# Output projection in products of 512 columns with one bank per chunk of tokens, its weights packed in fours, and the heads' reciprocal norms placed ahead on VectorE

## The chip, the cores and the metric

The kernel runs on one core of a Trainium2 chip. A core has TensorE (matrix products, written PE in the profile; its weight loads are the row PEld), VectorE (DVE), ScalarE (ACT), GpSimd (POOL) and SyncE (SP, which here issues all the transfers), each with its own queue, worked off in order. Matrix products write into PSUM, which has eight banks of 128 partitions x 512 float32 values; all else stands in SBUF or in HBM, and transfers (DMA) move it. The metric is the time of one execution on the device in microseconds; lower is better.

## The reference, cut to what matters

Two layers of an encoder trunk for 512 tokens of width 1024. In each layer one input projection of the residual stream x feeds three branches: a bidirectional state-space scan, differential attention with 8 heads, and cross-attention into 256 memory tokens. Each branch is projected to 1024 channels and weighted by a gate; the sum `merged` goes through one output projection and a layer norm. The lines that the change touches:

```python
o = _diff_attention(q, k, v, lam)
o = _rmsnorm(o, diff_norm_w[layer]) * (1.0 - lambda_init)   # one norm per head and token
y_diff = o.reshape(Bsz, S, DIFF_WIDTH) * jax.nn.silu(dg.astype(jnp.float32))
...
out = jnp.einsum('bsd,de->bse', merged, w_out[layer])
x = _layernorm(DEEPNORM_ALPHA * x.astype(jnp.float32) + out, ln_g[layer], ln_b[layer])
```

## The kernel before

**Arithmetic.** Every operand of a large product is split into a high and a low float32r part (`split`: ScalarE copies the high part, VectorE subtracts to get the low one), and `mm3` makes three products of each pair: low x high, high x low, high x high. Weights come from HBM in units of 128 x 1024 float32 (512 KB): the transfer fills `wr` (two buffers), the split fills `wh` and `wl` (three buffers each). `emit` runs through a plan of units and jobs and keeps loads and splits two units ahead.

**What sets the order.** A planner orders the instructions of each engine: among those that its own model holds ready, the one that stands first in the program goes first. `late(n)` moves the instructions in it n places back for that choice, `late(-n)` n places ahead. Between the first attention unit and `order.close` the queue of TensorE is not planned: it follows the program. All transfers wait in one queue of SyncE.

**The stages of a layer** are `ssd`, `cross`, `diff`, `wout`. In `diff` (from line 785) 35 steps s = 0 to 34 follow each other, each with one weight unit of 24 products of 512 columns (`proj2`): first the jobs `first`, then 12 products, then the jobs `amid`, then 12 products. The attention itself is in the jobs: `scores`, `turn` (transposes), `values`. `values(h, 1)` leaves the squares of head h in a tile of tag `fth` (two buffers), and `sums(h)` adds them up on TensorE; ScalarE copies the sums to `ss` (tile `fs` in the profile). `norm(lo, hi)` then makes the reciprocal norms of heads lo to hi-1 on VectorE: a reciprocal, then a chain of 16 small dependent instructions (`rsqrt` at line 113 is 12 of them; its result is tile `rs_y`).

- `norms`, in the middle of step 30: `norm` for the heads 0 to 6, a transpose on TensorE, a copy, a store to HBM (`rd`).
- `fin(h)` for h < 7: a transfer spreads the norms of head h from `rd` over 128 partitions into a tile of tag `fth`; VectorE multiplies `sdy` by it; the split gives `dy`, the operand of the branch's projection.
- `last`, in the middle of step 33: `norm` for head 7, whose sums are made at the start of that same step, and at once four products (`rb`, eight instructions on TensorE, named pm<-cst,rs_y) that spread it; `fin(7)` reads `rb` from PSUM.

After step s come the jobs `fin`: heads 0, 1 after step 31; 2, 3 after 32; 4, 5 after 33; 6, 7 after 34. Then `branch_out` projects `dy` in 8 units b(0) to b(7) of 24 products of 512 columns each, and `merged` splits the sum over the branches into the operands of the output projection.

**The output projection** (`wout`, from line 1029). The merged rows of 128 tokens are the operand that is loaded into TensorE, and the weight unit is streamed: `proj_tok` (line 182) makes products of 256 columns, so a unit holds 4 blocks of 128 rows x 256 columns, two units make a quarter of the output's columns, and two chunks of 128 tokens share a bank of tag `pj` (three buffers). When a quarter is complete, VectorE adds the residual (`stt`, line 1071; the residual comes by a transfer in `resid`, tags q1 and k0) and takes the statistics of 256 columns (line 1074). In layer 0 the four chunks go together, 8 units for the next layer's memory keys and values are put between the parts (`FILL`) and 8 more come behind them, and `norm` makes the layer norm and the transposed x for the next layer. In layer 1 (`GROUPS`) chunks 0 and 1 go first, then chunk 2, then chunk 3; the weights stay in SBUF, and `norm_last` writes each group out.

Of the kernel before, what the change touches and what calls it, by code (L numbers as in the profile page):

```python
# [15 lines left out]
ALU = mybir.AluOpType  # L16
# [4 lines left out]
P = 128  # L21
S = 512
D = 1024
KC = D // P
NL = 2
M = 256
EPS = 1e-5
ALPHA = (2 * NL) ** 0.25
# [13 lines left out]

LX, LD = 70, 80

FILL = (0, 2, 0, 2, 0, 4, 0, 0)

# [3 lines left out]
def bc(ap, shape):  # L52
    return ap.broadcast_to(shape)


class Net:
# [137 lines left out]
    def setup(self):  # L194
# [590 lines left out]
    def diff(self, l):  # L785
        nc = self.nc
# [184 lines left out]
        def job(fn, *a):  # L971
            return lambda: fn(*a)
# [10 lines left out]
        units = []  # L983
# [7 lines left out]
        for s, unit in enumerate(units):  # L991
            first = [job(scores, s + 1)] if s + 1 < nst else []
            amid = []
            if s % 4 == 2 and s < nst:
                amid.append(job(values, s // 4, 0))
            if s % 4 == 0 and 0 < s <= nst:
                amid.append(job(values, s // 4 - 1, 1))
            if s < nst:
                amid.append(job(turn, s))
            if s % 4 == 1 and 1 < s <= nst + 1:  # L1000
                first.append(job(sums, s // 4 - 1))
            if s == nst - 2:
# [26 lines left out]
    def wout(self, l, load, fill):  # L1029
# [3 lines left out]
        def begin():  # L1033
            op = self.op = self.fp
            self.rT = self.t(op, [P, 4, D], "dy0", bufs=1)
            if last:
                gb = self.t(op, [P, 4, D], "dy1", bufs=1)
                self.gb = [gb[:, i, :] for i in range(4)]
                nc.sync.dma_start(out=gb[:, 2:, :], in_=self.a["lngb"][l - 1:l].broadcast_to([P, 2, D]))
                nc.sync.dma_start(out=gb[:, :2, :], in_=self.a["lngb"][l:l + 1].broadcast_to([P, 2, D]))  # L1040
            else:
                load(op, "dy1", "rsw", "q0")
            self.st = self.t(op, [P, S], "ro", bufs=1)[:, :96].rearrange("p (c i e) -> p c i e", c=4, i=4)

        def resid(p, c, n):

            r = self.t(self.op, [P, n, 256], ("q1", "k0")[c // 2])
            src = self.a["x"] if l == 0 else self.nd
            e = slice(p * 256, (p + 1) * 256)
            nc.sync.dma_start(out=r, in_=src[c * P:(c + n) * P, e].rearrange("(c p) e -> p c e", c=n))  # L1050
            if l:
                for g, op in ((self.gb[2], ALU.mult), (self.gb[3], ALU.add)):
                    self.tt(r, r, bc(g[:, None, e], [P, n, 256]), op)
            return r

        def part(j, chunks):
            def f(wh=None, wl=None):
                p, half = j // 2, j % 2
                banks = [chunks[i:i + 2] for i in range(0, len(chunks), 2)]
                if half == 0:  # L1060
                    self.res = [resid(p, cs[0], len(cs)) for cs in banks]
                    self.ops = [self.bank(self.pj, "pj") for _ in banks]
                if wh is None:
                    wh, wl = self.wo[j]
                self.wo[j] = wh, wl
                self.proj_tok(half, wh, wl, *self.mg, self.ops, chunks)
                if half:
                    e = slice(p * 256, (p + 1) * 256)
                    for ps, r, cs in zip(self.ops, self.res, banks):
                        n = len(cs)  # L1070
                        self.stt(self.rT[:, cs[0]:cs[0] + n, e], ps[:, :n * 256].rearrange("p (c e) -> p c e", c=n), 0.5 / ALPHA,
                                 r, ALU.mult, ALU.add)
                        for c in cs:
                            nc.vector.bn_stats(out=self.st[:, c, p, :], in_=self.rT[:, c, e])
            return f

        def stats(chunks):
# [88 lines left out]
def pack(x, mem, positions, w_in, conv_w, conv_b, dt_bias, a_log, d_skip, ssd_norm_w, diff_lam, diff_norm_w,  # L1166
# [4 lines left out]
    def units(w):  # L1171
        return w.reshape(KC, P, -1, P).transpose(2, 1, 0, 3).reshape(-1, P, 1024)

    def pairs(w):
        return w.reshape(2, 4, P, -1, 256).transpose(3, 0, 2, 1, 4).reshape(-1, P, 1024)

    wu = []
    for l in range(NL):
        bs = w_br_ssd[l].reshape(4, 4, P, 4, 256).transpose(0, 3, 2, 1, 4).reshape(16, P, 1024)
        wi = np.concatenate([w_in[l][:, :5120], w_in[l][:, 5184:]], axis=1)  # L1180
        wu.append(np.concatenate([
            units(wi[:, :UV * P]), pairs(wi[:, UV * P:UDG * P]), units(wi[:, UDG * P:]),
            units(w_mem_kv[l][:, :D]), pairs(w_mem_kv[l][:, D:]), bs, units(w_br_diff[l]), units(w_br_cross[l]), pairs(w_out[l])]))
    chan = lambda v: v.reshape(-1, P).T
    pk = []
    for l in range(NL):
# [42 lines left out]
```

## Time and profile before

| what | us |
|---|---|
| median of 3 runs | 2241.68 (2237.81 to 2244.03) |
| the profiled execution, its own time | 2240.25 |
| its span, first to last instruction | 2238.5 |
| PE busy in the span | 2173.2 (97%) |
| DVE busy | 1589.9 (71%) |
| ACT busy | 1004.6 (45%) |
| mean granted clock of TensorE | 0.994 of full speed |

The page of the profile gives busy times of the engines, a picture of the span in 40 slices, the chain of work that ended last, and the costliest groups of instructions. A name such as pj<-wh,wT says that the product writes a tile of tag pj and reads tiles of the tags wh and wT; numbers at the end of a tag are left out (wT0 is wT, dy0 is dy). Products on PE are pipelined, so that the durations of neighbouring ones overlap: the time that one takes in a row of them is the distance from start to start. In lists by time, a bracket at the end of a row holds the idle time before it and what ended it.

### The profile page before, as it was taken

Reading aid. Unit: us, or ns where it says so; the run is one execution under the profiler, and the core shown is the slowest. Engines: PE = TensorE matmul, PEld = TensorE weight load, DVE = VectorE, ACT = ScalarE, POOL = GpSimd, SP = SyncE. Lnnn points to the kernel's source line nnn. Section 1 sums busy time; section 2 is a strip of 40 time slices with the busy share of each in tenths; the row PEclk is TensorE's granted clock in tenths of the full one; section 3 lists DMA queues with packets and bytes.
Section 4 is the critical chain, followed back from the end, with each engine's and each line's share of the span. In section 5 each row is a group of like instructions: output and inputs, shape, how many; then the busy total and the mean of one; then the engine's idle time right before and its main releaser. Section 6 shows DMA issues by size and latency. Waiting matters only on the chain.

```text
span 2238.5 us, 30344 instructions
## 1 busy us (share of the span) xinstructions
PE 2173.2 (97%) x11714; PEld 1787.8 (80%) x11714; DVE 1589.9 (71%) x2468; ACT 1004.6 (45%) x1895; POOL 52.9 (2%) x38
## 2 busy tenths in 40 slices
PE   8999999999999999998999999999999999999898
PEld 6777877788888788877996777787788887888678
DVE  7887888758544777765567888888744547777657
ACT  5664545424432555442355564554423325544430
POOL 0000000000000000000000000010100000000000
PEclk9999999999999999999999999999999999999999
DMA  4654444425453222233564545453433332223333
GB/s 148 180 160 144 147 142 138 126 85 190 145 179 115 90 81 82 81 104 108 163 225 115 165 141 151 132 152 122 123 124 118 116 106 85 78 84 90 109 99 128
DMA packets 108278, 283.79 MB, mean 127 GB/s; under 512 B 12588, under 2 KB 17252, under 8 KB 107876
## 3 DMA queue, kind: packets, MB, share of 16 engines
q1 hardware_dynamic: 108132, 281.84, 41.2%
q8 instruction: 92, 1.51, 0.3%
q14 instruction: 54, 0.44, 0.1%
HBM read 255.55 MB, written 17.85 MB: 122 GB/s over the span
## 4 chain that ended last, share of the span: by engine, by line
PE 71%; DVE 14%; DMA 7%; ACT 5%; issue 2%; SPq 0%; POOL 0%; DVEq 0%; POOLq 0%; ACTq 0%
PE pj L103 59%; PE pm L103 9%; DMA ab<-dab 4%; DVE wl L81 2%; PE pt L111 2%; DVE ab L81 2%; DVE acc L84 2%; ACT ab L91 1%; ACT wh L91 1%; DVE y L81 1%; DVE rx L81 1%; PE pt L103 1%; DMA wr<-wu 1%; DMA fth<-rd 1%; DVE yl L84 1%
## 5 line engine op out<-in xcount | busy, mean ns | idle before, releaser
L103 PE MATMUL pj<-xh,wl 128*128 128x512 f32 x1664 | 669.1, 402 | 10.8 <-DVE wl L81 8.9
L103 PE MATMUL pj<-xh,wh 128*128 128x512 f32 x1664 | 660.8, 397 | 0.0
L103 PE MATMUL pj<-xl,wh 128*128 128x512 f32 x1664 | 658.1, 395 | 0.0
L81 DVE TENSOR_TENSOR wl<-wr,wh 128x1024 fp32r<-128x1024 f32 x330 | 404.5, 1226 | 108.3 <-ACT wh L91 107.5
L91 ACT ACTIVATE wh<-wr 128x1024 fp32r<-128x1024 f32 x330 | 347.4, 1053 | 235.3 <-PE pj L103 199.5
L103 PEld LDWEIGHTS pj<-xh,wl 128*128 128x128 f32 x1664 | 314.1, 189 | 90.8 <-issue 18.3
L103 PEld LDWEIGHTS pj<-xh,wh 128*128 128x128 f32 x1664 | 313.7, 189 | 71.6 <-issue 6.0
L103 PEld LDWEIGHTS pj<-xl,wh 128*128 128x128 f32 x1664 | 314.1, 189 | 63.5 <-issue 3.6
L91 ACT ACTIVATE ab<-ab,bias 128x128 f32<-128x128 f32 x512 | 160.7, 391 | 121.9 <-DVE ab L81 121.3
L84 DVE SCALAR_TENSOR_TENSOR acc<-pj,hcw,acc 128x510 f32<-128x510 f32 x192 | 142.4, 743 | 23.8 <-ACT acc L91 22.4
L91 ACT ACTIVATE fpp<-pm,fmx 128x512 f32<-128x512 f32 x128 | 87.9, 687 | 83.4 <-DVE fmx L881 82.6
L881 DVE TENSOR_REDUCE fmx<-pm 128x1 f32<-128x512 f32 x128 | 87.0, 686 | 45.4 <-PE pm L103 45.1
L103 PE MATMUL pj<-yl,wh 128*128 128x512 f32 x256 | 102.3, 400 | 0.8 <-DVE yl L84 0.8
L103 PE MATMUL pj<-yh,wh 128*128 128x512 f32 x256 | 103.1, 403 | 0.0
L81 DVE TENSOR_TENSOR ab<-ab,cst 128x1024 f32<-128x1024 f32 x64 | 86.3, 1349 | 22.9 <-DMA ab<-dab 22.8
L103 PE MATMUL pj<-dy,wh 128*128 128x512 f32 (+1 forms) x384 | 101.9, 354 | 0.0
L103 PE MATMUL pj<-yh,wl 128*128 128x512 f32 x256 | 101.9, 399 | 0.0
L103 PE MATMUL pj<-cy,wh 128*128 128x512 f32 x256 | 78.8, 389 | 0.0
L103 PEld LDWEIGHTS pj<-dy,wh 128*128 128x128 f32 x384 | 68.0, 189 | 10.0
L103 PE MATMUL pj<-wh,xl 128*128 128x256 f32 x256 | 74.8, 292 | 0.0
L103 PE MATMUL pj<-wl,xh 128*128 128x256 f32 x256 | 72.4, 283 | 0.0
L103 PE MATMUL pj<-wh,xh 128*128 128x256 f32 x256 | 72.3, 283 | 0.0
(273 smaller groups left out, 3387.3 us busy)
## 6 DMA issues: line engine op xcount, KB each, us to landing
wr<-wu SPq DMA_DIRECT2D x336, 512.0 KB, 3.6
ab<-dab SPq DMA_DIRECT2D x64, 512.0 KB, 5.7
eb<-deb SPq DMA_DIRECT2D x64, 256.0 KB, 4.8
mkv<-dkv SPq DMA_DIRECT2D x16, 512.0 KB, 4.3
rsw<-rx SPq DMA_DIRECT2D x128, 64.0 KB, 2.0
dgt<-tg SPq DMA_DIRECT2D x18, 256.0 KB, 2.6
dkv<-mo SPq DMA_DIRECT2D x16, 256.0 KB, 4.0
dkv<-q SPq DMA_DIRECT2D x16, 256.0 KB, 3.7
```

Source lines behind the costliest of these rows:

```text
L81: (eng or self.nc.vector).tensor_tensor(out=out, in0=a, in1=b, op=op)
L84: self.nc.vector.scalar_tensor_tensor(out=out, in0=a, scalar=s, in1=b, op0=op0, op1=op1)
L91: self.nc.scalar.activation(out=out, in_=a, func=f, **kw)
L103: self.nc.tensor.matmul(out=out, lhsT=a, rhs=b, start=first, stop=last)
L111: self.nc.tensor.transpose(out=out, in_=x, identity=self.ident)
L881: nc.vector.tensor_reduce(out=mx[:, c:c + 1], in_=ps, axis=AX.X, op=ALU.min)
```

## The change

- **Weights.** `w_out` is packed by `quads`: a unit now holds 2 blocks of 128 rows x 512 columns, and four units make one half of the output's columns.
- **Products.** `out_tok` takes the place of `proj_tok` in `wout`: for each chunk of tokens, two row blocks of three products of 512 columns, into a bank of its own.
- **Banks.** These are of tag `pm` (four buffers) in place of `pj`. A chunk's sum is complete after four units (`quarter` 3); then one `stt` of 512 columns and one `bn_stats` of 512 columns follow for each chunk.
- **Residual.** One transfer for each chunk and half, 128 x 512, in the tags q1, rx (first half) and k0, k1 (second half).
- **Reciprocal norms.** `norm` becomes a job of its own, after step 29 for the heads 0 to 6 and after step 33 for head 7, in `late(-300)`; `spread` (the rest of `norms`) stays in the middle of step 30; `last` holds only the four spreading products and moves to the middle of step 34.
- **The jobs `fin`** now come two after step 32, three after step 33, three after step 34.

```diff
-LX, LD = 70, 80
+LX, LD, LN = 70, 80, 300
...
+    def out_tok(self, quarter, wh, wl, xh, xl, banks, chunks):
+
+        for o, c in zip(banks, chunks):
+            x = slice(c * P, (c + 1) * P)
+            for k in range(2):
+                kk, w = 2 * quarter + k, slice(k * 512, (k + 1) * 512)
+                self.mm3(o, xh[kk][:, x], xl[kk][:, x], wh[:, w], wl[:, w], kk == 0, kk == KC - 1)
...
         def norm(lo, hi):
 
-            n = 4 * (hi - lo)
             s0, ss = self.s0[:, 4 * lo:4 * hi], self.ss[:, 4 * lo:4 * hi]
-            nc.vector.reciprocal(out=s0, in_=s0)
-            self.stt(ss, ss, 1.0 / 128.0, s0, ALU.mult, ALU.mult)
-            self.tt(ss, ss, s0, ALU.mult)
-            self.ts(ss, ss, EPS, ALU.add)
-            r = self.rsqrt(self.fp, ss, n)
-            self.tt(r, r, s0, ALU.mult)
-            return r
-
-        def norms():
+            with self.late(-LN):
+                nc.vector.reciprocal(out=s0, in_=s0)
+                self.stt(ss, ss, 1.0 / 128.0, s0, ALU.mult, ALU.mult)
+                self.tt(ss, ss, s0, ALU.mult)
+                self.ts(ss, ss, EPS, ALU.add)
+                self.r = self.rsqrt(self.fp, ss, 4 * (hi - lo))
+                self.tt(self.r, self.r, s0, ALU.mult)
+
+        def spread():
 
             n = 4 * (KC - 1)
-            r = norm(0, KC - 1)
             pt = self.bank(self.pt, "pt")
-            self.tr(pt[:n, :P], r)
+            self.tr(pt[:n, :P], self.r)
...
         def last():
 
-            r = norm(KC - 1, KC)
+            r = self.r
             self.rb = self.bank(self.pm, "pm")
...
             if s == nst - 2:
-                amid.append(norms)
-            if s == nst + 1:
+                amid.append(spread)
+            if s == nst + 2:
                 amid.append(last)
             step(unit, first, amid)
-            if s >= nst - 1:
-                for h in range(2 * (s - nst + 1), min(2 * (s - nst + 1) + 2, KC)):
-                    self.T(job(fin, h))
+            if s in (nst - 3, nst + 1):
+                self.T(job(norm, *((0, KC - 1) if s < nst else (KC - 1, KC))))
+            for h in {nst: (0, 1), nst + 1: (2, 3, 4), nst + 2: (5, 6, 7)}.get(s, ()):
+                self.T(job(fin, h))
...
-        def resid(p, c, n):
-
-            r = self.t(self.op, [P, n, 256], ("q1", "k0")[c // 2])
+        def resid(p, c):
+
+            r = self.t(self.op, [P, S], (("q1", "rx"), ("k0", "k1"))[p][c // 2])
             src = self.a["x"] if l == 0 else self.nd
-            e = slice(p * 256, (p + 1) * 256)
-            nc.sync.dma_start(out=r, in_=src[c * P:(c + n) * P, e].rearrange("(c p) e -> p c e", c=n))
+            e = slice(p * S, (p + 1) * S)
+            nc.sync.dma_start(out=r, in_=src[c * P:(c + 1) * P, e])
...
-                p, half = j // 2, j % 2
-                banks = [chunks[i:i + 2] for i in range(0, len(chunks), 2)]
-                if half == 0:
-                    self.res = [resid(p, cs[0], len(cs)) for cs in banks]
-                    self.ops = [self.bank(self.pj, "pj") for _ in banks]
+                p, quarter = divmod(j, 4)
+                if quarter == 0:
+                    self.res = [resid(p, c) for c in chunks]
+                    self.ops = [self.bank(self.pm, "pm") for _ in chunks]
...
-                self.proj_tok(half, wh, wl, *self.mg, self.ops, chunks)
...
+                self.out_tok(quarter, wh, wl, *self.mg, self.ops, chunks)
+                if quarter == 3:
+                    e = slice(p * S, (p + 1) * S)
+                    for ps, r, c in zip(self.ops, self.res, chunks):
+                        self.stt(self.rT[:, c, e], ps, 0.5 / ALPHA, r, ALU.mult, ALU.add)
+                        nc.vector.bn_stats(out=self.st[:, c, p, :], in_=self.rT[:, c, e])
...
+    def quads(w):
+        return w.reshape(4, 2, P, -1, 512).transpose(3, 0, 2, 1, 4).reshape(-1, P, 1024)
```

More of the change, by code (lines that the diff above doesn't have):

```diff
@@ L1042, in begin @@
                 load(op, "dy1", "rsw", "q0")
-            self.st = self.t(op, [P, S], "ro", bufs=1)[:, :96].rearrange("p (c i e) -> p c i e", c=4, i=4)
-        def resid(p, c, n):
-            r = self.t(self.op, [P, n, 256], ("q1", "k0")[c // 2])
+            self.st = self.t(op, [P, S], "ro", bufs=1)[:, :48].rearrange("p (c i e) -> p c i e", c=4, i=2)
+        def resid(p, c):
+            r = self.t(self.op, [P, S], (("q1", "rx"), ("k0", "k1"))[p][c // 2])
             src = self.a["x"] if l == 0 else self.nd
-            e = slice(p * 256, (p + 1) * 256)
-            nc.sync.dma_start(out=r, in_=src[c * P:(c + n) * P, e].rearrange("(c p) e -> p c e", c=n))
+            e = slice(p * S, (p + 1) * S)
+            nc.sync.dma_start(out=r, in_=src[c * P:(c + 1) * P, e])
             if l:
                 for g, op in ((self.gb[2], ALU.mult), (self.gb[3], ALU.add)):
-                    self.tt(r, r, bc(g[:, None, e], [P, n, 256]), op)
+                    self.tt(r, r, g[:, e], op)
             return r
@@ L1065, in f @@
                 self.wo[j] = wh, wl
-                self.proj_tok(half, wh, wl, *self.mg, self.ops, chunks)
[L1067 to L1074, printed above, removed]
+                self.out_tok(quarter, wh, wl, *self.mg, self.ops, chunks)
[4 more added lines that the diff above has]
+                        nc.vector.bn_stats(out=self.st[:, c, p, :], in_=self.rT[:, c, e])
             return f
@@ L1182, in pack @@
             units(wi[:, :UV * P]), pairs(wi[:, UV * P:UDG * P]), units(wi[:, UDG * P:]),
-            units(w_mem_kv[l][:, :D]), pairs(w_mem_kv[l][:, D:]), bs, units(w_br_diff[l]), units(w_br_cross[l]), pairs(w_out[l])]))
+            units(w_mem_kv[l][:, :D]), pairs(w_mem_kv[l][:, D:]), bs, units(w_br_diff[l]), units(w_br_cross[l]), quads(w_out[l])]))
     chan = lambda v: v.reshape(-1, P).T
```

## The prediction

> **What bounds the kernel now.** I read the page first, then the stages, then the waits of TensorE, then lists by time.
>
> ```profile
> span 2238.5 us, 30344 instructions
> PE 2173.2 (97%) x11714; PEld 1787.8 (80%) x11714; DVE 1589.9 (71%) x2468; ACT 1004.6 (45%) x1895; POOL 52.9 (2%) x38
> PE 71%; DVE 14%; DMA 7%; ACT 5%; issue 2%; SPq 0%; POOL 0%; DVEq 0%; POOLq 0%; ACTq 0%
> ```
>
> TensorE is busy 2173.2 of 2238.5 us, so all that can be won without removing products is 65.3 us of idle time and what products lose to a slow clock. The stages that the change touches (columns: length, then busy time of PE, PEld, DVE, ACT, POOL, granted clock, share and rate of the transfers):
>
> ```profile
> 985.00:1026.00 41.00, 31.52 (x146) 26.39 (x147) 18.86 (x39) 14.17 (x23) 0.00 (x0) 0.92 0.31 97
> 1068.00:1144.00 76.00, 75.64 (x640) 75.33 (x638) 44.55 (x77) 26.08 (x33) 0.00 (x0) 1.00 0.55 173
> 1144.00:1172.00 28.00, 27.17 (x193) 24.89 (x194) 19.43 (x28) 18.36 (x28) 0.52 (x1) 1.00 0.73 246
> 1172.00:1824.00 652.00, 638.35 (x3127) 510.56 (x3126) 470.69 (x666) 297.35 (x585) 26.82 (x16) 1.00 0.44 132
> ```
>
> The output projection of layer 0 (second row) is bound by TensorE alone. The end of `diff` (first row) is not: 9.5 of 41 us are idle, at a lower clock. The waits of TensorE (total, times, longest) say on whom:
>
> ```profile
> engine line waited for: us in total, times, longest us
> PE pm L103 <- DVE rs_y L81: 16.1, 2, 8.2
> PE pj L103 <- DVE wl L81: 9.9, 5, 6.8
> ```
>
> The largest wait of the kernel is the four products of `last` on the reciprocal norms of head 7, once in each layer. By time, layer 0, then layer 1:
>
> ```profile
> 1002.01 0.95 PE L103 MATMUL pt<-cst,fth 128*128 128x1 f32 x8
> 1005.44 0.39 PE L103 MATMUL pj<-xh,wh 128*128 128x512 f32 x1
> 1013.99 2.08 PE L103 MATMUL pm<-cst,rs_y 128*128 128x128 f32 x8 [8.16 <-DVE rs_y L81]
> 1016.29 0.63 PE L103 MATMUL pj<-xl,wh 128*128 128x512 f32 x1
> 1016.72 0.63 PE L103 MATMUL pj<-xh,wh 128*128 128x512 f32 x1
> 1024.95 0.39 PE L103 MATMUL pj<-dy,wl 128*128 128x512 f32 x1
> ...
> 2121.04 0.39 PE L103 MATMUL pj<-xh,wh 128*128 128x512 f32 x1
> 2129.38 2.08 PE L103 MATMUL pm<-cst,rs_y 128*128 128x128 f32 x8 [7.96 <-DVE rs_y L81]
> 2140.74 0.39 PE L103 MATMUL pj<-dy,wl 128*128 128x512 f32 x1
> ```
>
> The sums of head 7 start at 1002.01, the first half of step 33 ends at 1005.67 (1005.44 + 0.23), and then the queue stands until 1013.99. After that the products come 0.43 us apart (1016.29 to 1016.72) instead of 0.227, for the clock has fallen:
>
> ```profile
> 1014.00:1018.00 4.00, 4.00 (x14) 3.57 (x15) 1.20 (x2) 0.63 (x1) 0.00 (x0) 0.53 0.00 0
> ```
>
> **The change, part by part.**
>
> *1. The wait in `last` (removed).* From the end of the first half of step 33 to the first product of b(0): layer 0, 1024.95 - 1005.67 = 19.28 us; layer 1, 2140.74 - 2121.27 = 19.47. In that time TensorE has 36 products of 512 columns and the eight instructions of `rb` to do. The pitch of warm products, and the cost of a small instruction:
>
> ```profile
> 1068.48 0.28 PE L103 MATMUL pj<-wh,fpp 128*128 128x256 f32 x1
> 1074.08 0.28 PE L103 MATMUL pj<-wh,v 128*128 128x256 f32 x1
> ...
> 992.08 0.44 PE pt L111 x4
> ```
>
> From 1024.95 to 1068.48 are the 192 products of b(0) to b(7): 0.2267 us each. Four transposes took 0.44 us, so eight small instructions come to some 0.9. Needed: 36 x 0.2267 + 0.9 = 9.06 us. Lost: 10.2 and 10.4 us, **20.6 in all**, of which 16.1 are the wait and 4.5 the slow clock behind it. Neither has other work beside it.
>
> The Trainium skill ("TensorE: Matmul & The Clock Gate", section "Part 1: The HAM clock gate") says that an idle window of about 3.4 us halves the clock, and that as long a busy one restores it. The 0.53 over 4 us behind 8.16 us of idle agrees. By that rule a wait that shrinks below 3.4 us loses its slow stretch too.
>
> *2. What is late next: `last` in step 34.* It now stands 24 products later, so TensorE comes to `rb` at 1005.67 + 24 x 0.2267 = 1011.1 (layer 1: 2126.7). VectorE and ScalarE before:
>
> ```profile
> 1004.26 0.16 ACT L91 ACTIVATE fs<-pt 128x4 f32<-128x4 f32 x1
> 1003.88 1.23 DVE L81 TENSOR_TENSOR wl<-wr,wh 128x1024 fp32r<-128x1024 f32 x1 [0.87 <-ACT wh L91]
> 1006.44 0.69 DVE L81 TENSOR_TENSOR sdy<-sdy,fth 128x512 f32<-128x512 f32 x1 [0.74 <-DMA fth<-rd]
> 1007.05 0.16 DVE L84 SCALAR_TENSOR_TENSOR fs<-fs,fs 128x4 f32<-128x4 f32 x1
> 1010.91 0.69 DVE L81 TENSOR_TENSOR sdy<-sdy,fth 128x512 f32<-128x512 f32 x1 [0.45 <-DMA fth<-rd]
> 1013.17 0.69 DVE L81 TENSOR_TENSOR dy<-sdy,dy 128x512 fp32r<-128x512 f32 x1
> 1013.78 0.15 DVE L81 TENSOR_TENSOR rs_y<-rs_y,fs 128x4 f32<-128x4 f32 x1
> ...
> 974.65 0.18 DVE L84 SCALAR_TENSOR_TENSOR fs<-fs,fs 128x28 f32<-128x28 f32 x1
> 979.22 0.19 DVE L81 TENSOR_TENSOR rs_y<-rs_y,fs 128x28 f32<-128x28 f32 x1
> ```
>
> The sums are there at 1004.42. The chain of 16 took 6.9 us (1007.05 to 1013.93), because it started behind a multiply of `fin` that waited for a transfer, and shared VectorE with others of the kind; for the heads 0 to 6 the same 16 took 4.8 us (974.65 to 979.41), with other work between. Bounds for the wait at the new place: below, the chain goes ahead from 1005.1, when the weight split ends, takes 4.8, is done at 9.9: no wait. Above, everything on VectorE stays as it was: 1013.93 - 1011.1 = 2.8 us (2.6 in layer 1). I take 0.5 per layer, nearer the lower end, because three of the multiplies of `fin` now stand behind the chain in the program. **+1.0**; if the cover is gone, +5.4.
>
> Queued behind the chain on VectorE are multiplies and splits of `fin`. The last transferred one ended its split at 1013.86. TensorE now reaches b(0) at 1005.67 + 9.06 = 1014.7 and uses row block k of `dy` after 3k products: block 6 at 1018.8, block 7 at 1019.5. Block 7 follows `rb` (done 1012.0) by a multiply and a split of some 0.7 each: near 1014. So the heads have 5 us in hand, if their transfers don't move. Each of them takes over 3 us and they share two buffers; their places in the plan go back by up to a step (5.44 us), their readiness doesn't. That is priced below as a rival.
>
> *3. Norms of heads 0 to 6, hoisted.* Before, their chain was done at 979.41, and the transpose that needs it came at 986.3: no wait to remove. Its 16 instructions now come before others that are ready, the reductions of `scores` among them. They took their time among the same neighbours before, 0.18 to 0.19 us each, and a step's 24 products (5.44 us) hide it. Cost: 0; cover gone: 16 x 0.19 = 3 us per layer.
>
> *4. Products of 512 columns.* 48 products of 256 columns went from 1068.48 to 1074.08: 0.1167 us each. A layer has 384 of them: 44.8 us. After: 192 x 0.2267 = 43.5 us. Saved 1.3 us per layer, **-2.5 in all**. The row of 1068 to 1144 has TensorE idle for 0.36 us, so the saving lies on the path there; bounds 0 (the fills behind it are paced by the weights' transfers: 0.73 of their time in 1144 to 1172) and 2.6.
>
> The skill's same page (section "Back-to-back issue gap") gives a warm gap of N/2.4 + 2.5 ns. By it a pair of 256 would lose 2.5 ns to one of 512, an estimate of 1.0 us over 384 pairs instead of 2.5. The trace's gap is larger (6.7 ns), and the trace decides.
>
> *5. Banks, evictions, residual.* A bank's last six products take 1.36 us, and its eviction on VectorE about as long (0.69 for the `stt`, some 0.7 for the statistics), so the evictions keep step; two fill units (2.8 us each) stand between parts 3 and 4, so the second half finds its banks free. In layer 1 the second half of group 0 takes the other two banks. Residual transfers: 8 instead of 8 in layer 0; all tiles of layer 1 have their own buffer. VectorE's total falls (8 statistics of 512 for 16 of 256 per layer). Cost 0; cover gone: one eviction, 1.4 us, per half.
>
> *6. The tail of layer 1.* Behind the last product:
>
> ```profile
> 2228.95 0.28 PE L103 MATMUL pj<-wh,wT 128*128 128x256 f32 x1
> 2229.27 0.42 DVE L84 SCALAR_TENSOR_TENSOR dy<-pj,k 128x256 f32<-128x256 f32 x1 [0.52 <-PE pj L103]
> 2229.73 0.43 DVE L1074 BATCH_NORM_STATS2 ro<-dy 128x6 f32<-128x256 f32 x1
> ...
> 1136.52 0.69 DVE L84 SCALAR_TENSOR_TENSOR dy<-pj,k 128x512 f32<-128x512 f32 x1 [1.02 <-PE pj L103]
> ```
>
> The `stt` doubles: 0.42 to 0.69. Statistics of 512 columns aren't in the trace: between 0.43 and 0.86 (two of 256); 0.70 by the same growth as the `stt`. **+0.5** on the path; the end of layer 0 grows alike, but under 8 fill units of 2.8 us.
>
> **Sum.** -20.6 + 1.0 - 2.5 + 0.5 = -21.6. The profiled execution's time is 2240.25 us (span 2238.5 and 1.75 around it), so 2218.6; it lies 1.4 under the median of the runs (2241.68, from 2237.81 to 2244.03), which would give 2220. I say **2219**.
>
> **Rivals.**
>
> *A. The chain stays behind `fin` (15%).* VectorE keeps its order, `rb` waits 2.8 and 2.6 us: 2223, or 2227 if the slow clock (4.5) returns as well. For: the multiply at 1006.44 blocked VectorE for a transfer, and a place in a list doesn't shorten that. Against: the chain has 5.4 us more, and place 300 ahead.
>
> *B. `dy` becomes the wait (9%).* The transfers of `fin` follow their places and come two steps late (10.9 us): the last split ends at 1024.7 instead of 1013.86, while TensorE wants it at 1018.8: 6 us per layer, 2231. For: two buffers, shared with the squares of head 7. Against: they are issued when a buffer is free, not when the program comes to them.
>
> *C. The wait only moves (6%).* TensorE stands at b(0) as long as it did at `rb`; then only parts 4 and 6 are left, 2238. It takes the transfers to be the true limit, 5 + 8 us later than now.
>
> *D. Slower by the clock (2%).* Each unit now goes through twice as many banks as before (four in layer 0), with six products for each. If TensorE paused at each change and the clock fell, a product of 512 columns would take 0.43 instead of 0.227: over all 384 products +77 us, 2295; from some 108 slow products on, the gain is gone. Against: two banks alternate in 1068 to 1144, at a clock of 1.00 and 0.36 us idle. The skill has this as a rule on that page, "A second HAM failure mode: psum-queue depth-cycling".
>
> *E. Slower by the planner (3%).* TensorE's order in the next `ssd` is planned anew. Its idle time there is 13.7 us (652 less 638.35); to use up the gain, it would have to grow to 35: near 2245. Smaller shifts, some 4 us either way, belong to the range.
>
> **How the numbers follow.** Forecast 65%, A 15%, B 9%, C 6%, D 2%, E 3%. The forecast's own range is 2213 to 2223 (no wait, or A's upper wait, with the runs' own spread of 3 us); with A and much of B I give **2211 to 2231**. A measurement of this kernel can tell 0.3%, 6.7 us: under 2235 is faster, over 2248 slower. The forecast, A and most of B are faster: 0.88; C and the rest of B the same: 0.07; D and E slower: 0.05.
>
> **What would show it.** Right: no row of TensorE's waits on rs_y above 1 us; clock 1.00 where 0.53 stood; some 10 us between `rb`'s old place and b(0) gone in both layers; output products 0.227 us apart; the last `stt` at 0.69. Wrong: a wait on `dy` at b(0), a wait on rs_y over 2 us in step 34, products of `wout` waiting for a bank, or a gain before 985 or between 1172 and 1824.

## The result, and the profile after

| what | before | after |
|---|---|---|
| median of 5 runs, us | 2242.17 (2237.81 to 2244.36) | 2220.13 (2217.3 to 2223.68) |
| ratio, 95% interval | | 0.9904 (0.9889 to 0.9919) |
| span of the profiled execution, us | 2238.5 | 2221.9 |
| mean granted clock | 0.994 | 0.997 |

The kernel is 22.0 us faster; 2219 was forecast. The profiled execution of after, at 2223.68, was the slowest of its five, so sums made from its trace come out smaller than the medians say. Two executions of all that were measured, one of before (9087.02) and one of a variant below (4342.89), took two to four times as long as the rest and are left out of the ratios. The head of the page of after, then the rows that answer to the first and the last of the prediction's table, the first at the same times, the last about where that stage now lies (columns as there):

```profile
span 2221.9 us, 29523 instructions
PE 2171.0 (98%) x11330; PEld 1768.0 (80%) x11330; DVE 1585.9 (71%) x2440; ACT 1004.3 (45%) x1895; POOL 54.2 (2%) x38
```

```profile
985.00:1026.00 41.00, 38.98 (x194) 32.21 (x193) 23.49 (x48) 17.07 (x26) 0.00 (x0) 1.00 0.37 111
...
1166.00:1807.00 641.00, 629.26 (x3090) 503.93 (x3089) 467.49 (x660) 295.73 (x584) 27.60 (x16) 1.00 0.45 133
```

TensorE is busy for as long as before (2171.0 against 2173.2 us) although it now issues 384 products fewer: the narrow ones that went were replaced at no gain, as will be seen. What shrank is above all the idle time, from 65.3 to 50.9 us. In the first row it is 2.0 us where it was 9.5, and the clock is 1.00 where it was 0.92. The waits of TensorE (total, times, longest):

```profile
PE pj L103 <- DVE wl L81: 10.1, 5, 6.9
...
PE pm L103 <- DVE rs_y L81: 1.6, 2, 1.0
```

The wait on rs_y fell from 16.1 to 1.6 us. The list by time of TensorE in after, from the sums of head 7 to the end of the output projection, layer 0 and then layer 1, and below it the two rows of before that its layer 1 is compared with:

```profile
1005.28 0.95 PE L103 MATMUL pt<-cst,fth 128*128 128x1 f32 x8
...
1014.38 0.39 PE L103 MATMUL pj<-dy,wl 128*128 128x512 f32 x1
...
1016.42 0.39 PE L103 MATMUL pj<-dy,wl 128*128 128x512 f32 x1
1017.35 1.16 PE L103 MATMUL pm<-cst,rs_y 128*128 128x128 f32 x8 [0.54 <-DVE rs_y L81]
1018.26 0.48 PE L103 MATMUL pj<-xh,wl 128*128 128x512 f32 x1
...
1062.72 0.39 PE L103 MATMUL pm<-wh,fpp 128*128 128x512 f32 x1
...
1130.28 0.40 PE L103 MATMUL pm<-wh,wT 128*128 128x512 f32 x1
...
2109.58 0.61 PE L103 MATMUL pt<-cst,fth 128*128 128x1 f32 x5
...
2122.15 1.16 PE L103 MATMUL pm<-cst,rs_y 128*128 128x128 f32 x8 [1.04 <-DVE rs_y L81]
...
2167.46 0.39 PE L103 MATMUL pm<-xh,fpp 128*128 128x512 f32 x1
...
2212.02 0.39 PE L103 MATMUL pm<-wh,wT 128*128 128x512 f32 x1
```

```profile
2117.61 0.84 PE L103 MATMUL pt<-cst,fth 128*128 128x1 f32 x7
...
2184.27 0.28 PE L103 MATMUL pj<-xh,fpp 128*128 128x256 f32 x1
```

From the sums to the first product of the output projection:

| layer | before | after | gain |
|---|---|---|---|
| 0 | 1068.48 - 1002.01 = 66.47 | 1062.72 - 1005.28 = 57.44 | 9.03 |
| 1 | 2184.27 - 2117.61 = 66.66 | 2167.46 - 2109.58 = 57.88 | 8.78 |

That is 17.8 us in the two stages where the prediction looked for it. The other stages of the same two executions: the start to the sums of layer 0, +3.3; the output projections from first to last product, 67.56 for 67.72 in layer 0 and 44.57 for 44.68 in layer 1, so -0.3 together from start to start (a last product of 512 columns is itself 0.12 us longer than one of 256, so that with it counted 0.05 is left); from there to the first unit of layer 1, +1.0; that unit to the sums of layer 1, -3.2; behind the last product, +0.4. With -17.8 they make the -16.6 between the two spans. The +3.3 and -3.2 lie almost wholly in stages that the change does not touch: of the +3.3, 0.3 falls between the sums of the first head and those of the last, where norms were moved, and 1.7 is a stretch of slow clock (454 to 458 us at 0.57, where before has 1.00) of the kind described at the end. Other executions give other values there: the start to the sums of layer 0 took 1002.5 us in a second profiled execution of the same changed kernel, 1005.3 here.

The table also holds a surprise. In after, ten products of b(0) stand ahead of `rb` (from 1014.38 to 1016.65, three to each 0.68 us), and the rest of step 34 behind it. TensorE therefore comes to the waiting place 2.3 us later than the program's order would bring it there. The list of VectorE in the same stretch says how much that hides:

```profile
1008.29 0.15 DVE L84 SCALAR_TENSOR_TENSOR fs<-fs,fs 128x4 f32<-128x4 f32 x1
1008.36 0.69 DVE L81 TENSOR_TENSOR dy<-sdy,dy 128x512 fp32r<-128x512 f32 x1
...
1013.13 0.16 DVE L84 SCALAR_TENSOR_TENSOR rs_y<-rs_q,rs_y 128x4 f32<-128x4 f32 x1
1013.97 0.69 DVE L81 TENSOR_TENSOR sdy<-sdy,fth 128x512 f32<-128x512 f32 x1 [0.68 <-DMA fth<-rd]
...
1014.65 1.22 DVE L81 TENSOR_TENSOR wl<-wr,wh 128x1024 fp32r<-128x1024 f32 x1
...
1017.14 0.16 DVE L81 TENSOR_TENSOR rs_y<-rs_y,fs 128x4 f32<-128x4 f32 x1
```

The chain took 9.0 us, from 1008.29 to 1017.30, not the 4.8 assumed and not even the 6.9 of before. It began 2.0 us earlier behind the start of the sums than before (3.0 for 5.0) and ended at the same distance (12.0 for 11.9). Multiplies, splits of `dy` and a weight split stand between its links, and one multiply held it for its transfer. Had `rb` followed the first half of step 34 at once, at 1014.38, it would have waited some 3 us (1017.35 - 1014.38).

The tail, as VectorE's list has it:

```profile
2212.45 0.69 DVE L84 SCALAR_TENSOR_TENSOR dy<-pm,k 128x512 f32<-128x512 f32 x1 [3.27 <-PE pm L103]
2213.18 0.69 DVE L1077 BATCH_NORM_STATS2 ro<-dy 128x6 f32<-128x512 f32 x1
```

Statistics of 512 columns take 0.69 us; 0.70 was estimated.

### The profile page after: what moved, and what is told of

The parts are those of the page before. It is cut to its first block, busy times and chain, and to the rows that moved or that the text cites. A ratio compares the mean times of both kernels' runs of the same rounds, so it can differ in the third digit from the quotient of the medians.

```text
span 2221.9 us, 29523 instructions
## 1 busy us (share of the span) xinstructions
PE 2171.0 (98%) x11330; PEld 1768.0 (80%) x11330; DVE 1585.9 (71%) x2440; ACT 1004.3 (45%) x1895; POOL 54.2 (2%) x38
## 4 chain that ended last, share of the span: by engine, by line
PE 71%; DVE 14%; DMA 8%; ACT 5%; issue 1%; POOL 0%; SPq 0%; POOLq 0%; DVEq 0%; ACTq 0%
PE pj L103 55%; PE pm L103 13%; DMA ab<-dab 5%; DVE wl L81 3%; PE pt L111 2%; DVE ab L81 2%; DVE acc L84 2%; ACT ab L91 1%; ACT wh L91 1%; DMA wr<-wu 1%; DVE y L81 1%; DVE rx L81 1%; PE pt L103 1%; DMA fth<-rd 1%; DVE m L81 1%
## 5 line engine op out<-in xcount | busy, mean ns | idle before, releaser
L81 POOL TENSOR_TENSOR sqa<-sqa,sz 128x512 f32<-128x512 f32 x32 | 52.9, 1654 | 845.6 <-ACT sz L91 845.6
```

The source lines that it names most:

```text
L81: (eng or self.nc.vector).tensor_tensor(out=out, in0=a, in1=b, op=op)
```

## The experiments

Medians are in us; a ratio is against runs of the kernel before on the same chip, with its 95% interval. "Stage" is the time from the sums of head 7 to the first product of the output projection (before 66.47 and 66.66, after 57.44 and 57.88).

**The two parts alone.** First the norms' part with the output projection of before:

```diff
     # of the change, kept: norm, spread, last, the places of the jobs fin
-    out_tok, quads, banks pm, residuals of 512 columns
+    proj_tok, pairs, banks pj, residuals of 256 columns
```

> The norms' part of the change alone (norm ahead, spread, last in step 34, the later fin jobs); the output projection, its banks, residuals and packing are those of before. Theory 1 (the trace of the changed kernel: its 512-column products in the output projection are 0.2333 us apart, twice the 0.1167 us of the 256-column ones, so the projection gained nothing): this kernel takes as long as the changed one, 2218 to 2224, and from the sums of head 7 to the first product of the output projection 57 to 58 us per layer instead of 66.5. Theory 2 (the prediction): it lacks the 2 us that the projection was to give: 2222 to 2225. Theory 3 (the projection gave some 4 us, by which the medians' gain of 22 exceeds the 17.8 us that the two stages show): 2224 to 2227.

Measured: 2220.39 (2217.22 to 2225.36), ratio 0.9913 (0.9899 to 0.9928). Stage 57.63 and 58.13. Its wait on rs_y:

```profile
PE pm L103 <- DVE rs_y L81: 1.6, 2, 1.3
```

Then the reverse, the output projection's part with the norms of before:

```diff
-    norm as a job in late(-LN), spread, last in step 34
+    norms in the middle of step 30, last with its norm in step 33, fin as before
```

> The output projection's part alone (512-column products, bank per chunk, quads, residuals); norms, last and fin as before. Theory 1: no gain, 2240 to 2244, the wait of TensorE on rs_y is 16 us as before, products of the output projection 0.233 us apart. Theory 2: 2 us less than before, 2239 to 2241. Theory 3: 4 us less, 2236 to 2239.

Measured: 2236.21 (2234.53 to 2239.45), ratio 0.9983 (0.9975 to 0.9992). Stage 67.17 and 66.13, and the wait is whole:

```profile
PE pm L103 <- DVE rs_y L81: 16.7, 2, 8.6
```

So the norms' part makes 20.2 of the 22 us by itself, and the other part some 4 of 2240 (its interval goes from 1.8 to 5.6); that the two add up to 24.5 and not 22.0 lies within their intervals. The 4 us are of the size forecast for the products (2.5), but they are not in the products: the output projection of layer 0 takes 67.56 us from first to last product here, against 67.72 with the products of before. Where they are is taken up below.

**Place in the program, or place ahead?** The change does two things to the norm of head 7: it moves `last` to step 34, and it puts the chain 300 places ahead. One kernel keeps the second without the first, with `last` where it was:

```diff
-            if s == nst + 2:
+            if s == nst + 1:
+                first.append(job(norm, KC - 1, KC))
                 amid.append(last)
...
-            if s in (nst - 3, nst + 1):
-                self.T(job(norm, *((0, KC - 1) if s < nst else (KC - 1, KC))))
+            if s == nst - 3:
+                self.T(job(norm, 0, KC - 1))
```

> The changed kernel with last back in the middle of step 33, and the norm of head 7 issued at that step's start right behind its sums, 300 places ahead. Theory 1 (the place of last is what won): TensorE waits again, 4 to 8 us per layer on rs_y, with a slow clock behind it: 12 to 20 us slower than the changed kernel. Theory 2 (the norms ahead are what won): within 3 us of the changed kernel.

Measured: 2237.16 (2234.68 to 2241.02), ratio 0.9988 (0.9979 to 0.9997). Stage 66.97 and 67.12: nothing is gained there. Of its waits, and of its stretch behind the wait in layer 0 (columns as in the table of stages):

```profile
PE pm L103 <- DVE rs_y L81: 16.6, 2, 8.6
```

```profile
1014.00:1018.00 4.00, 4.00 (x16) 3.30 (x16) 3.50 (x6) 1.90 (x3) 0.00 (x0) 0.69 0.00 0
```

The wait is back in full, and the slow clock behind it with it. The other kernel does the first without the second:

```diff
-LX, LD, LN = 70, 80, 300
+LX, LD, LN = 70, 80, 0
```

> The changed kernel with LN = 0: norm is still a job of its own behind steps 29 and 33, but has no place ahead. Theory 1 (moving last by half a step and more is what won, the place ahead does little, because the chain waits for the copy of the sums and for multiplies of fin that stand before it anyway): within 2 us of the changed kernel, TensorE waits on rs_y 1 to 4 us in all. Theory 2 (the place ahead is what brings the chain through): the chain falls behind the multiplies of fin and ends up to 3 us later per layer: 3 to 8 us slower than the changed kernel.

Measured: 2216.01 (2214.24 to 2219.02, three executions), ratio 0.9893 (0.9876 to 0.9909), which can't be told from the changed kernel. Stage 59.11 and 58.63, 1.7 and 0.8 longer than in after. TensorE's list shows what stands there instead:

```profile
1010.33 0.39 PE L103 MATMUL pj<-dy,wl 128*128 128x512 f32 x1
...
1014.12 0.73 PE L103 MATMUL pj<-dy,wl 128*128 128x512 f32 x2 [0.53 <-ACT dy L91]
...
1016.49 0.73 PE L103 MATMUL pj<-dy,wh 128*128 128x512 f32 x2 [1.18 <-DVE dy L81]
...
1017.35 1.16 PE L103 MATMUL pm<-cst,rs_y 128*128 128x128 f32 x8
```

More products of b(0) have slipped ahead of `rb`, 19 in place of 10, so many that they meet rows of `dy` that aren't ready; `rb` itself waits no more. The gain is thus the later place of `last`; the place ahead on VectorE is worth a microsecond in its stage, and in the whole it doesn't show.

**Do the transfers of `fin` follow their places?** That was rival B. All eight jobs were put behind step 34:

```diff
-            for h in {nst: (0, 1), nst + 1: (2, 3, 4), nst + 2: (5, 6, 7)}.get(s, ()):
+            for h in {nst + 2: range(KC)}.get(s, ()):
```

> The changed kernel with all eight jobs fin put behind step 34. Theory 1 (transfers go when they are ready and a buffer is free, not when the program comes to them; the heads have some microseconds in hand): within 2 us of the changed kernel, the last transferred head's split ends at about the same distance behind the sums of head 7 (17 us). Theory 2 (the prediction's rival B: the transfers follow their places): the split of that head ends some 11 us later, TensorE waits on dy in the first unit of the projection of that branch: 4 to 8 us more per layer, 8 to 16 in all.

Measured: 2220.78 (2219.79 to 2222.0), ratio 0.9908 (0.989 to 0.9925). Stage 58.17 and 57.45, in all within 0.3 us of after, with no wait on `dy` over 0.2 us in the list of waits; the transfers start at the same distances from the sums as in after, to 0.8 us.

That does not test rival B, though, for the change had moved the transfers already. They share the two buffers of `fth` with the squares of head 7, which take theirs in the middle of step 32. Before, the jobs of heads 0 and 1 stood ahead of these squares in the program; in after, and in the kernel with all eight at the end, every job stands behind them. The first and the last of the seven transfers of layer 0 (SP, at their issue), in before and in after:

```profile
988.30 0.82 SPq L954 DMA_DIRECT2D fth<-rd  x2
...
1007.16 0.99 SPq L954 DMA_DIRECT2D fth<-rd  x2
```

```profile
1001.88 5.21 SPq L960 DMA_DIRECT2D fth<-rd  x3
...
1017.25 0.32 SPq L960 DMA_DIRECT2D fth<-rd  x1
```

From the start of the sums, the first comes at -13.7 us in before and at -3.4 in after, the seventh (in before the second of its row) at 5.8 and at 12.0. What hangs on the seventh in after, VectorE's multiply and split and then TensorE:

```profile
1021.22 0.69 DVE L81 TENSOR_TENSOR sdy<-sdy,fth 128x512 f32<-128x512 f32 x1
1022.62 0.69 DVE L81 TENSOR_TENSOR dy<-sdy,dy 128x512 fp32r<-128x512 f32 x1 [0.70 <-ACT dy L91]
```

```profile
1022.91 0.39 PE L103 MATMUL pj<-dy,wl 128*128 128x512 f32 x1
1023.36 0.73 PE L103 MATMUL pj<-dy,wh 128*128 128x512 f32 x2
```

Its split ends at 1023.31, 18.0 us behind the start of the sums (18.5 in layer 1), where before it was 11.9 (1013.86 - 1002.01). TensorE's next product comes 0.05 us later, 0.45 us behind its forerunner in place of 0.23: too short a wait for the list, but it is the one that counts. Eight traces have this part of the change: after, its repetition, the kernel with the norms' part alone, this one and four more below. In both layers of each, the last split ends 17.6 to 18.7 us behind the first row of the sums, and the output projection begins 39.4 to 39.5 us after that; 173 products of 0.2267 us, 39.2, lie between. The wait on rs_y in these 16 stages goes from 0.3 to 1.3 us and does not show in their lengths. So the transfers did move back with their places, as rival B has it, though by 6.2 us and not by 10.9, and the last of them is what now ends the stage. Whether heads 0 and 1 put back ahead of the squares would win anything was not tried.

**Width of the products.** Two products of 256 columns for each of 512, in the new banks and the new packing, and beside it the changed kernel once more:

```diff
-                kk, w = 2 * quarter + k, slice(k * 512, (k + 1) * 512)
-                self.mm3(o, xh[kk][:, x], xl[kk][:, x], wh[:, w], wl[:, w], kk == 0, kk == KC - 1)
+                kk = 2 * quarter + k
+                for i in range(2):
+                    w, e = slice(k * 512 + i * 256, k * 512 + (i + 1) * 256), slice(i * 256, (i + 1) * 256)
+                    self.mm3(o[:, e], xh[kk][:, x], xl[kk][:, x], wh[:, w], wl[:, w], kk == 0 and i == 0,
+                             kk == KC - 1 and i == 1)
```

> The changed kernel with each product of 512 columns in the output projection made as two products of 256 columns into the halves of the same bank; packing, banks, residuals and norms stay. Theory 1 (the width of the products is worth nothing here, 0.2333 us against 2 x 0.1167): the stage from the first to the last product of the projection takes 67.6 us in layer 0 and 44.6 in layer 1 as with 512 columns, and the time is the changed kernel's within 1.5 us. Theory 2 (the prediction's pitch of 0.2267 for 512, so that 256-column products cost 1.3 us more per layer): 2.5 us slower than the changed kernel.

> The changed kernel once more, beside the next three, as the mark for differences of a few microseconds. Theory 1 (norms -18 to -20, output projection -2 to -4 on top, seen in the medians of its part alone): 2217 to 2221, and from the end of layer 0's output projection to the sums of head 7 in layer 1 some 3 us less than before. If that stretch comes out as in the kernel before (981), the 4 us of the projection's part were a matter of single runs.

Measured: 2221.16 (2217.53 to 2221.52), ratio 0.9907 (0.9891 to 0.9923), and 2218.62 (2217.43 to 2220.26), ratio 0.99 (0.9884 to 0.9916). The chain of waits has the same piece of the output projection in both: one unit of the halves, and one of after, with the whole of layer 1 under it:

```profile
1058.16 11.20 PE pm L103 x96
```

```profile
1062.88 11.19 PE pm L103 x48
...
2167.62 44.81 PE pm L103 x192
```

96 products of 256 columns take as long as 48 of 512: 0.1167 us and 0.2333 us each. The two medians can't be told apart either. In b(0) to b(7) the same width took 0.2267. The step of the prediction that carried the pitch of b(0) over to the output projection is wrong.

**Why 0.2333?** Three variants in one kernel. In layer 0 the operand that is loaded is the layer's input (`xh`, `xl`), not the merged rows. In layer 1, chunk 2 makes its three products in another order, and chunk 3 loads the weights and streams the merged rows. So layer 0 and chunk 3 compute something other than the output projection:

```diff
+        if len(chunks) == 4:
+            xh, xl = self.rows(self.xh, self.xl)
...
+            if chunks in ((2,), (3,)):
+                ...
+                    if c == 2:
+                        self.mm(o, xh[kk][:, x], wh[:, w], kk == 0, False)
+                        self.mm(o, xh[kk][:, x], wl[:, w], False, False)
+                        self.mm(o, xl[kk][:, x], wh[:, w], False, kk == KC - 1)
+                    else:
+                        self.mm3(o, wh[:, v], wl[:, v], xh[kk], xl[kk], kk == 0, kk == KC - 1)
```

> For the distance between products alone; it changes what the output projection computes. Layer 0: the operand that is loaded is x instead of the merged rows. Layer 1, chunks 0 and 1: as in the changed kernel. Chunk 2: the three products of a pair in the order high x high, high x low, low x high. Chunk 3: the weights are the loaded operand (a block of 128 x 128), the merged rows are streamed. Theory 1 (the 0.2333 us belong to the tiles that hold the merged rows when they are loaded): 0.227 in layer 0 and in chunk 3, 0.233 in chunks 0 to 2. Theory 2 (they belong to weights that are streamed): 0.233 in layer 0 and chunks 0 to 2, 0.227 in chunk 3. Theory 3 (the order of the three): 0.227 in chunk 2 alone.

Measured (2219.99 in the one run): in layer 0, by the chain, 0.2267 us each; in layer 1 all three groups stay at 0.2333. From the chain, and from TensorE's list in chunk 3:

```profile
1060.62 10.88 PE pm L103 x48
```

```profile
2201.30 0.40 PE L103 MATMUL pm<-wT,xh 128*128 128x512 f32 x1
...
2202.00 0.40 PE L103 MATMUL pm<-wT,xh 128*128 128x512 f32 x1
```

The slower pitch goes with the operand of merged rows, whether it is loaded or streamed. None of the three expectations had that whole. Two causes remain, what the rows hold or where they lie, and two kernels tell them apart. In layer 0, nobody reads the layer's input any more by then, so its tiles can take the merged rows:

```diff
+            if l == 0:
+                self.mg = self.rows(self.xh, self.xl)
+                self.split(self.mg[0][j], self.mg[1][j], self.mrg[:, j, :])
+                return
             fp, self.mg = self.fp, mgs
```

> In layer 0 the two parts of the merged rows are written into the tiles of the layer's input (xh, xl), which nobody reads any more, and not into wT, fpp and v; the values, the order and the streamed weights stay. Theory Place (the slower pitch belongs to the tiles' place): products of layer 0 come 0.2267 us apart, as with x in e7, the first to the last in 66.3 us and not 67.56, and the whole is some 1.3 us below the changed kernel, near 2218. Theory Values (it belongs to what is multiplied): 0.2333 as before, 67.56, and the time of the changed kernel (2219 to 2220). Layer 1 stays as it is under both: 44.57.

And the opposite, the layer's input in the tiles of the merged rows:

```diff
+            if l == 0:
+                self.act(mgs[0][j], self.xh[:, j, :])
+                self.ts(mgs[1][j], self.xl[:, j, :], 1.0, ALU.mult)
+                return
             self.split(mgs[0][j], mgs[1][j], self.mrg[:, j, :])
```

> The opposite: in layer 0 the tiles wT, fpp and v are filled with the two parts of the layer's input (copied from xh and xl), not with those of the merged rows, so the output projection of layer 0 multiplies other values in the same tiles and everything behind it computes something else. Theory Place: 0.2333 us apart in layer 0. Theory Values: 0.2267. The time itself tells nothing here.

Measured: the merged rows in the tiles of x (2217.59, 2214.5 to 2218.85, ratio 0.9892 from 0.9878 to 0.9907), and x in the tiles of the merged rows (2219.9 in one run). The chain's first unit in each:

```profile
1057.04 10.88 PE pm L103 x48
...
2158.42 44.81 PE pm L103 x192
```

```profile
1059.06 11.19 PE pm L103 x48
```

Merged rows in xh and xl: 0.2267 us each, and the output projection of layer 0 takes 66.39 us, not 67.56; layer 1, which kept its tiles, stays at 44.81 for 192. Input in wT, fpp and v: 0.2333. So it is the tiles, not the values. What about them does it was not tried. The median with the rows in xh and xl is 1.0 under that of the changed kernel's second run, but the intervals overlap: the 1.2 us are shown by the trace and not by the times.

**The 4 us of the second part.** The output projection's part alone again, with the norms of before, but in products of 256 columns:

```diff
     # as e2 (norms of before), with the two products of 256 columns for each of 512 shown above
```

> The norms of before, and the output projection's new banks, residuals and weights, but with two products of 256 columns for each of 512. e2_wout_only, the same with 512, stood 4 us below the kernel before (2236.2 against 2240.5), with nothing of it in the products. Theory Wide (fewer and wider products make room for something later): 2240 here. Theory Layout (banks, evictions or transfers of the new layout): 2236 here too, and layer 1's ssd from its first product to the sums of head 7 near 947 us, not 950 to 952.

Measured: 2239.91 (2237.7 to 2244.11, 11 runs), ratio 0.9996 (0.9987 to 1.0005), against 0.9983 (0.9975 to 0.9992) with 512 columns. By the medians the gain goes with the width of the products, as the first theory had it, and new banks, evictions, residuals and packing alone give nothing. But the two intervals overlap and the two kernels ran on different chips, so that this is likely and not shown; in its favour, the kernel with `last` in step 33, which has the wide products and the whole wait, also lies 3.4 us under before. And the sign by which the trace was to tell the two apart, the length of layer 1 from its first unit to the sums of head 7, failed: it took 945.6 us here, where the gain is gone, and 946.4 with 512 columns (952.1 in before). In all twelve other traces it is 944.9 to 949.9, so that the single trace of before is the one that stands apart. A place where 512 columns save 4 us is therefore not shown. The traces give 0.05 us in the products themselves, and the rest moves between stages from one profiled execution to the next by more than is sought. It stays open.

## Why the prediction was right

*Step 1, the wait in `last`: right in place and mechanism, nearly right in size.* The wait and the slow clock behind it are gone from both layers, and no other wait of that size has come. 20.6 us less 1.0 for what is late next made 19.6; the two stages gave 17.8. The least that the stage can take, by the prediction's own terms, is 48 products and 192 at 0.2267, and 0.8 and 0.9 for the small instructions: 56.1. After needs 57.44 and 57.88, so 1.3 and 1.8 us remain. In layer 0, TensorE spends 0.7 of them at the wait on rs_y (from 1016.65 to 1017.35), 0.1 in the 36 products before it (8.29 us for 8.16) and 0.5 in the 194 behind it (44.46 for 43.98). What holds it is the last split of `dy`: it ends at 18.0 and 18.5 us where the least stage wants it at 16.7 (56.1 less 39.4), which is these 1.3 and 1.8 us. By these numbers, TensorE without the wait on rs_y would have stood at the split instead.

*Step 2, what is late next: the sum held, the reason did not.* Forecast were 0.5 us per layer, measured 0.54 and 1.04. But the forecast had the chain run ahead of the multiplies and take 4.8 us, and the chain took 9.0. VectorE did what rival A said. Its price did not come due, because ten ready products of b(0) stood ahead of `rb` on TensorE. That TensorE keeps the program's order there, as the prediction took it, is an assumption that failed, and it failed to the good: that 1.0 came out near its forecast is luck. A second one failed to the bad. The transfers' places go back, "their readiness doesn't", it says; but the split of the last transferred head came 6.2 and 6.8 us later behind the sums, so the 5 us in hand were used up, and `dy`, which has no term in the sum, ends the stage. The kernel without the place ahead met `dy` earlier, after more products of b(0), and waited up to 1.2 us at once.

*Step 3, norms of heads 0 to 6: right.* From the first sums to those of head 7, 226.25 us of layer 0 became 226.55, and 226.14 of layer 1 became 226.42.

*Step 4, products of 512 columns: the term that was mis-sized.* -2.5 was forecast; -0.28 was measured from first to last start, and nothing (0.05) with the last product counted, which is the lower of the two bounds named there. The pitch of 0.2267 was read from b(0), whose operands lie in other tiles; in the tiles of the merged rows 512 columns take exactly twice 256. The estimate by the Trainium skill ("TensorE: Matmul & The Clock Gate", section "Back-to-back issue gap"), -1.0, was too large as well. The part alone does run some 4 us faster, so that the total came out close for a reason that the prediction doesn't contain.

*Step 5, banks and evictions: right.* No wait of TensorE on a bank of the output projection, and the new banks with narrow products (e10) can't be told from before, 0.9996.

*Step 6, the tail: right.* +0.36 from the start of the last product, of which 0.11 is its own width, for +0.5 forecast.

*The rivals.* A: its cause came, its price did not. B: its cause came in part, 6 us in place of 10.9, and at a smaller price, at most 1.3 and 1.8 us in place of 6 per layer. C fell with the stages, though a part of the wait did move to `dy`. D: the clock stood at 1.00 through the output projection of layer 0:

```profile
1062.00:1138.00 76.00, 76.00 (x451) 67.04 (x450) 42.12 (x69) 25.31 (x34) 0.00 (x0) 1.00 0.54 163
```

E: the next `ssd` got no slower; its row above has 11.7 us idle, for 13.7 in the row of before, which is 11 us longer, and layer 1 from its first unit to its sums took 948.9 us for 952.1.

*The balance.* -17.8 in the stages, -0.3 in the products, +0.4 in the tail make -17.7; the runs say -22.0. The remaining 4 us are as large as what the output projection's part gives by its runs alone, and as unplaced. So the mechanism of the large term, the wait and its slow clock, was right and shown; that 2219 lies so near 2220.13 is in part luck, because the stages and the products gave 4 us less than forecast and something unplaced gave as much more.

## What to carry to other kernels

When an engine stands on a chain of small instructions of another, look first for a later place of the consumer with ready work before it: moving the consumer by 24 products gave the gain here, and putting the chain 300 places ahead gave none without it. Where transfers share buffers with other work, look at the order in which the program takes the buffers: two transfers that fell behind one tile made the last operand 6 us later, and a test of that must change this order. Read the pitch of an operation from rows with the same operand tiles, not only the same shape. And when a planner may fill the place before a wait, count what stands ready behind it: that work, and not the chain alone, set how long TensorE waited.

## What the runs showed of the hardware

**The pitch of a product hangs on the tiles of its operand.** Same shape, same type, same clock of 1.00: 0.2267 us with x's tiles or b(0)'s, 0.2333 with wT, fpp and v, with either content, loaded or streamed. Products of 256 columns do not follow: they take 0.1167 us in the output projection of before, and 0.120 in the attention (the median of the 352 products pm<-wT,v of after, tiles of two of the same tags). What of the tiles does it stays open.

**Behind a wait of 1.2 us another 1.7 can be lost.** Isolated stretches of slow clock occur in stages that the change doesn't touch, and not in each execution. In `cross`, TensorE waits 1.2 us on `sqa` and then makes eight products of one column. After, then its repetition, at the same instructions of layer 1:

```profile
1607.27 1.18 PE L103 MATMUL pt<-cst,sqa 128*128 128x1 f32 x8 [1.21 <-POOL sqa L81]
```

```profile
1608.00:1612.00 4.00, 4.00 (x13) 3.23 (x14) 2.00 (x13) 0.05 (x1) 0.00 (x0) 0.57 0.07 27
```

```profile
1602.82 1.05 PE L103 MATMUL pt<-cst,sqa 128*128 128x1 f32 x8 [1.20 <-POOL sqa L81]
```

```profile
1603.00:1607.00 4.00, 3.89 (x23) 3.13 (x24) 2.01 (x13) 1.08 (x2) 0.00 (x0) 1.00 0.19 78
```

The same wait, followed once by some four microseconds at 0.57 (0.43 x 4 = 1.7 us lost) and once by none. Over the 13 traces this place comes 26 times, once in each layer, and 15 times the clock behind it stood at 0.57 for 4 us. The Trainium skill ("TensorE: Matmul & The Clock Gate", section "Part 1: The HAM clock gate") says that the window over which activity is judged runs freely, and that the moment at which the clock changes depends on where in the window the first product falls. That fits a stretch that comes and goes; but its figure, an idle window of about 3.4 us, is longer than the gap seen here, and no run shows which part of the eight small products counts as idle. Each such stretch moves an execution by as much as the smaller effects of this case, which is one reason why single traces could not place the last 4 us.
